# A trunk layer on one core: the gate and feed-forward products taken as 512, 256 and 384 columns over high and low token parts that lie side by side

## The chip, the core and the metric

The kernel runs on one core of a Trainium2 chip. The metric is the device time of one execution in microseconds (us). The median of three runs before the change is 2050.86 us (2049.79 to 2052.56). The engines are called as the profile calls them: PE is TensorE's matmul and PEld its weight load, DVE is VectorE, ACT is ScalarE, POOL is GpSimd, SP is SyncE, whose queue issues nearly all DMAs.

## What is computed

One transformer-like layer over 384 tokens of width 2048: 128 context tokens (the prompt) and 256 latent tokens. All of it is float32.

```
def trunk_layer(x, cond, lw, attend):
    sh1, sc1, g1, sh2, sc2, g2 = modulation(cond, w_mod_l, b_mod_l)
    h = rms_norm(x, n1) * (1 + sc1) + sh1
    q, k, v, u = project_in(h, w_in_l, qg_l, kg_l)
    attn = attend(q, k, v)
    x = x + g1 * token_mixing(h, attn, u, w_na_proj_l, w_fnet_proj_l, w_gate_l, w_o_l)
    h2 = rms_norm(x, n2) * (1 + sc2) + sh2
    x = x + g2 * swiglu(h2, w_gu_l, w_down_l)
    return x, k, v

def token_mixing(h, attn, u, w_na_proj, w_fnet_proj, w_gate, w_o):
    na = attn.reshape(b, t, D_NA) @ w_na_proj
    fn = fourier_mix(u) @ w_fnet_proj
    g_na, g_fn = jnp.split(jax.nn.sigmoid(h @ w_gate), 2, axis=-1)
    return (g_na * na + g_fn * fn) @ w_o

def swiglu(h, w_gate_up, w_down):
    a, g = jnp.split(h @ w_gate_up, 2, axis=-1)
    return (jax.nn.silu(g) * a) @ w_down
```

The change bears on `h @ w_gate` (2048 by 4096) and on `h @ w_gate_up` (2048 by 11264).

## The kernel before

**High and low parts.** A float32 matrix is split into a high part H, rounded to the type fp32r, and a low part L = x - H (`split`, L142 to L144: a cast on ACT, a subtraction on DVE). A product of two float32 matrices is then three fp32r products added up in PSUM: H by H, H by L and L by H (`mm3`, L146 to L149; the fourth, L by L, is left out). In `mm3` the second argument is the stationary operand, 128x128, and the third streams past it. The first two products have the same stationary operand. The profile names the streaming operand first: `mm<-hL,wh` is wh stationary and hL streaming.

**Weights.** All weight matrices come through one list of units in the order of their use (`units`). A unit is two row blocks by 512 columns (512 KB): loaded by SP into `wraw` (four buffers, L187), split into `wh` and `wl` (three buffers each) in `split_unit`, used by PE. `next_unit` is called once for each unit of products: it splits a later unit, lets the other work of the stage take its paced steps (`Paced`: rows of the modulation, attention, splits of activations), and asks for one more load. So the order on ACT, DVE and SP is fixed by the place of each call in the Python text, and each engine takes its instructions in that order.

**PSUM.** Accumulators are tiles of 128 partitions by 512 float32 columns, one bank each. From the mixing stage on, `acc_tile` hands out seven of them in rotation (`new_ring`); the gate stage takes its four from the four `mm` tiles alone.

**Stages**, by the time at which their products stand in the trace: the input projection (to 333 us), where tokens are stationary and 512 weight columns stream; the gates (to 676), eight times eight units, in which the Fourier and attention branches are woven by `front`; the mixing stage (to 811), the two branch projections, each gated; the output projection (to 948); the feed-forward part. There `FF_PARTS` cuts 44 blocks of 128 hidden channels into parts of 8, 8, 8, 8, 8 and 4. In a part, groups of four channel blocks take two halves of eight units (half 1: the SiLU branch, half 0: the factor), and then the part's rows of `w_down` are applied in units of 512 columns with the activations (`cH`, `cL`) stationary. The very first group (to 1018 us) uses the unnormed tokens with two more columns (386 wide, `wide`, `late_norm`); it is not touched by the change. From then on `h2` is there as `hH` and `hL`.

**What the change touches.** In the gates and in the later feed-forward groups the weights are stationary and the 384 tokens stream, so that the result has channels on partitions and tokens in columns. `new_h` (L232) gives the two token tiles of a row block, each 128x384. In the gate loop (L1018 to L1036) a result of 384 columns is copied out of PSUM (`gst`, L1032) by ACT, or by DVE for two of the four tiles in some of the rounds, and stored in DRAM (`s_gate`, by ACT's queue). `load_gates` (L1053) loads four results at once in the mixing stage, a sigmoid is taken at the third unit (L1084), the product with the branch follows (L1092). In the feed-forward part a result goes through SiLU on ACT (L1319) or a multiplication on DVE (L1321), straight from PSUM. `split_act` (L1248) then splits the activations; in the last part, which has four blocks, its step stands directly behind each multiplication (`work.step()`), elsewhere it is spread over the following units.

Of the kernel before, what the change touches and what calls it, by code (L numbers as in the profile page):

```python
# [19 lines left out]
P = 128  # L20
# [12 lines left out]
CH = 512  # L33
# [68 lines left out]
def trunk_kernel(ctx: ExitStack, tc: tile.TileContext, io: dict):  # L102
# [35 lines left out]
    def nm(s):  # L138
        return f"{s}{next(ids)}"
# [6 lines left out]
    def mm3(out, aH, aL, bH, bL, start, stop):  # L146
        nc.tensor.matmul(out, aH, bH, start=start, stop=False)  # L147
        nc.tensor.matmul(out, aH, bL, start=False, stop=False)  # L148
        nc.tensor.matmul(out, aL, bH, start=False, stop=stop)  # L149

    def warm_sqrt():

        warm = small.tile([P, 1], F32, tag="warm", bufs=1, name=nm("warm"))
        nc.scalar.activation(out=warm, in_=ones[:, 0:1], func=AF.Sqrt)
# [72 lines left out]
    rq = consts.tile([P, NT, NH], F32, tag="rq", name="rq")  # L227

    hH = [None] * KT
    hL = [None] * KT  # L230

    def new_h(kt):  # L232
        hH[kt] = hpool.tile([P, TOK], F32R, tag=f"tH{kt}", name=nm(f"hH{kt}_"))
        hL[kt] = hpool.tile([P, TOK], F32R, tag=f"tL{kt}", name=nm(f"hL{kt}_"))
        return hH[kt], hL[kt]

    s_qkvu = [dram.tile([P, NT, CH], F32, tag=f"sq{i}", name=f"s_qkvu{i}") for i in range(8)]
    s_gate = [dram.tile([P, 4, TOK], F32, tag=f"sg{i}", name=f"s_gate{i}") for i in range(8)]
    s_row = {
# [26 lines left out]
    with ExitStack() as ph:  # L266
# [751 lines left out]
        for fc8 in range(8):  # L1018
            po = [mm_tile() for _ in range(4)]
            sts = []  # L1020
            for u in range(0, KT, 2):
                wH, wL = next_unit()
                for f in range(4):
                    s = slice(f * P, (f + 1) * P)
                    if f == 2:
                        mid_unit()
                    for kk in range(2):
                        k = u + kk
                        mm3(po[f][:, :TOK], wH[:, kk, s], wL[:, kk, s], hH[k], hL[k], k == 0, k == KT - 1)
                    if u == KT - 2:  # L1030
                        st = gst.tile([P, TOK], F32, tag="st", name=nm("gst"))
                        (nc.vector.tensor_copy if f < 2 and any(soft) else nc.scalar.copy)(st, po[f][:, :TOK])  # L1032
                        sts.append(st)
# [19 lines left out]
        def load_gates(f4, i):  # L1053
            g = bs.tile([P, 4, TOK], F32, tag="gl", bufs=3, name=nm("gl"))
            nc.sync.dma_start(g, s_gate[i * 4 + f4])
            return g
# [19 lines left out]
        for f4 in range(4):  # L1076
            gl = [None, None]
            for i, bH, bL in ((1, fH, fL), (0, aH, aL)):
                _, gl[i] = gates.take()
                po = [acc_tile() for _ in range(4)]  # L1080
                for u in range(0, 8, 2):
                    wH, wL = next_unit()
                    if u == 4:
                        nc.scalar.activation(out=gl[i], in_=gl[i], func=AF.Sigmoid)  # L1084
                    for f in range(4):
# [170 lines left out]
    def late_norm(o, sg, half):  # L1256
# [10 lines left out]
        return b  # L1267

    def silus(sg, bs):
        for f, b in enumerate(bs):  # L1270
# [19 lines left out]
    for part, nf in enumerate(FF_PARTS):  # L1290
# [5 lines left out]
        for c4 in range(nf // 4):  # L1296
            for half in (1, 0):
                po = [acc_tile() for _ in range(4)]
                bs = []
                for u in range(0, KT, 2):  # L1300
                    wH, wL = next_unit()
                    for f in range(4):
                        s = slice(f * P, (f + 1) * P)
                        for kk in range(2):
                            k = u + kk
                            xH, xL = wide(k) if facc is None else (hH[k], hL[k])
                            mm3(
                                po[f][:, : xH.shape[1]], wH[:, kk, s], wL[:, kk, s], xH, xL, k == 0, k == KT - 1
                            )
                        if u < KT - 2:  # L1310
# [5 lines left out]
                        if facc is None:  # L1316
                            bs.append(late_norm(po[f], sg[:, f], half))
                        elif half:
                            nc.scalar.activation(out=sg[:, f], in_=po[f][:, :TOK], func=AF.Silu)  # L1319
                        else:  # L1320
                            nc.vector.tensor_mul(sg[:, f], sg[:, f], po[f][:, :TOK])  # L1321
                            if nf == 4:
                                work.step()
# [84 lines left out]
```

## Time and profile before

| | |
|---|---|
| median of three runs | 2050.86 us |
| the profiled execution | 2052.19 us |
| its span in the trace | 2050.4 us |
| input projection and modulation, 0 to 335 us | PE busy 318.77 us |
| gates, Fourier and attention, 335 to 676 us | PE busy 337.80 us |
| mixing, 676 to 810 us | PE busy 134.00 us |
| output projection, 810 to 987 us | PE busy 176.23 us |
| feed-forward, 1018 to 2013 us | PE busy without a gap |
| last down projection, 2013 to 2050.4 us | PE busy 33.01 us |

In the page and the views, a group's line gives busy time, mean ns of one instruction, then the engine's idle time ahead of it and what ended it. A row of the timeline is start, duration, engine, line, what is written and read, and shape. A row of the windows view gives, for a stretch, its length, each engine's busy time with its number of instructions in brackets, the granted clock of PE, the share of time that the DMA engines worked, and GB/s. A matmul's duration holds its latency; consecutive ones overlap, so that the distance of two starts is what one costs.

### The profile page before, as it was taken

What the parts mean: (1) busy time and instruction counts of PE and PEld (TensorE: products, weight loads), DVE (VectorE), ACT (ScalarE), POOL (GpSimd) and SP (SyncE); (2) the same over time, 40 slices, a digit from 0 to 9 for tenths busy, and PEclk for the clock granted to TensorE, in tenths of its full rate; (3) what the DMA queues carried; (4) which work ended last, traced back from release to release, by engine and by line L of the source; (5) the groups of instructions that cost most, each with busy time, mean ns of one, the idle gap of its engine ahead of it and who ended that gap; (6) DMA issues with size and microseconds to landing.
All of it is one profiled execution on the core that took longest, in us unless ns stands there. A gap on an engine that the chain in (4) does not pass through costs nothing.

```text
span 2050.4 us, 27528 instructions
## 1 busy us (share of the span) xinstructions
PE 2025.8 (99%) x10986; PEld 1843.8 (90%) x10986; DVE 1248.0 (61%) x1528; ACT 757.9 (37%) x1135; POOL 43.1 (2%) x92
## 2 busy tenths in 40 slices
PE   7999999999999999999999999999999999999999
PEld 4668788999999999889998999899989998999897
DVE  4746889788987777765854444545454334333456
ACT  4433232456665434334523332222222232223222
POOL 1000000000001000010000000000000000000000
PEclk9999999999999999999999999999999999999999
DMA  9996979677776776754455555455554444444453
GB/s 332 328 338 222 309 232 315 215 217 212 228 212 181 258 248 194 250 168 154 124 167 156 152 163 155 144 153 155 155 163 134 124 129 127 129 128 123 136 163 123
DMA packets 220384, 390.46 MB, mean 190 GB/s; under 512 B 28464, under 2 KB 77632, under 8 KB 220256
## 3 DMA queue, kind: packets, MB, share of 16 engines
q1 hardware_dynamic: 213088, 382.13, 59.5%
q10 hardware_dynamic: 4672, 6.31, 0.9%
q8 instruction: 86, 1.41, 0.3%
q0 software_dynamic: 2496, 0.27, 0.1%
q14 instruction: 42, 0.34, 0.1%
HBM read 371.81 MB, written 20.51 MB: 191 GB/s over the span
## 4 chain that ended last, share of the span: by engine, by line
PE 94%; DMA 3%; DVE 2%; ACT 1%; issue 0%; SPq 0%; ACTq 0%; DVEq 0%
PE mm L147 19%; PE mm L149 19%; PE mm L148 19%; PE at L147 11%; PE at L149 11%; PE at L148 11%; PE at L404 1%; DMA wm<-in_w_mod 1%; DMA wraw<-in_w_in 1%; PE at L893 1%; PE at L979 1%; PE at L958 1%; DMA wmr<-in_w_mod 1%; DVE accr L329 0%; DMA xc<-in_x_prompt 0%
## 5 line engine op out<-in xcount | busy, mean ns | idle before, releaser
L144 DVE TENSOR_TENSOR wl<-wraw,wh 128x1024 fp32r<-128x1024 f32 (+1 forms) x464 | 559.1, 1205 | 668.5 <-ACT wh L143 667.3
L143 ACT CAST wh<-wraw 128x1024 fp32r<-128x1024 f32 (+1 forms) x464 | 480.9, 1038 | 1032.0 <-PE at L148 272.9
L147 PE MATMUL mm<-hH,wh 128*128 128x384 f32 x1152 | 389.4, 338 | 2.4 <-DVE gst L1032 2.4
L149 PE MATMUL mm<-hH,wl 128*128 128x384 f32 x1152 | 385.5, 335 | 0.0
L148 PE MATMUL mm<-hL,wh 128*128 128x384 f32 x1152 | 385.2, 334 | 0.0
L329 DVE SCALAR_TENSOR_TENSOR accr<-wmr,csz,accr 128x1024 f32<-128x1024 f32 x240 | 304.8, 1278 | 5.2 <-DMA wmr<-in_w_mod 5.1
L147 PEld LDWEIGHTS mm<-hH,wh 128*128 128x128 f32 x1152 | 216.3, 188 | 8.1 <-issue 4.3
L148 PEld LDWEIGHTS mm<-hL,wh 128*128 128x128 f32 x1152 | 216.4, 188 | 0.0
L149 PEld LDWEIGHTS mm<-hH,wl 128*128 128x128 f32 x1152 | 216.2, 188 | 0.0
L147 PE MATMUL at<-hH,wh 128*128 128x384 f32 x640 | 213.9, 334 | 0.0
L149 PE MATMUL at<-hH,wl 128*128 128x384 f32 x640 | 213.9, 334 | 0.0
L148 PE MATMUL at<-hL,wh 128*128 128x384 f32 x640 | 213.8, 334 | 0.0
L147 PE MATMUL mm<-wh,hH 128*128 128x512 f32 x404 | 160.8, 398 | 1.9 <-ACT hH L548 1.2
L148 PE MATMUL mm<-wl,hH 128*128 128x512 f32 x404 | 158.1, 391 | 2.8 <-DVE wl L144 2.8
L149 PE MATMUL mm<-wh,hL 128*128 128x512 f32 x404 | 158.4, 392 | 0.7 <-DVE hL L144 0.4
L147 PE MATMUL mm<-wh,cH 128*128 128x512 f32 x352 | 137.1, 389 | 0.0
L149 PE MATMUL mm<-wh,cL 128*128 128x512 f32 x352 | 137.0, 389 | 0.0
L148 PE MATMUL mm<-wl,cH 128*128 128x512 f32 x352 | 137.0, 389 | 0.0
L147 PEld LDWEIGHTS at<-hH,wh 128*128 128x128 f32 x640 | 120.1, 188 | 1.0 <-ACT wh L143 0.8
L148 PEld LDWEIGHTS at<-hL,wh 128*128 128x128 f32 x640 | 120.1, 188 | 0.2
L149 PEld LDWEIGHTS at<-hH,wl 128*128 128x128 f32 x640 | 120.1, 188 | 0.0
L147 PEld LDWEIGHTS mm<-wh,hH 128*128 128x128 f32 x404 | 76.0, 188 | 25.6 <-issue 3.1
(283 smaller groups left out, 2633.5 us busy)
## 6 DMA issues: line engine op xcount, KB each, us to landing
wraw<-in_w_gate_up SPq DMA_DIRECT2D x176, 512.0 KB, 3.7
wmr<-in_w_mod SPq DMA_DIRECT2D x128, 512.0 KB, 4.9
wraw<-in_w_down SPq DMA_DIRECT2D x88, 512.0 KB, 3.7
wraw<-in_w_gate SPq DMA_DIRECT2D x64, 512.0 KB, 4.3
wm<-in_w_mod SPq DMA_DIRECT2D x80, 384.0 KB, 6.7
wraw<-in_w_in SPq DMA_DIRECT2D x56, 512.0 KB, 5.8
wraw<-in_w_o SPq DMA_DIRECT2D x32, 512.0 KB, 4.7
wraw<-in_w_fnet_proj SPq DMA_DIRECT2D x16, 512.0 KB, 4.9
```

The source lines that it names most:

```text
L143: nc.scalar.copy(H, x)
L144: nc.vector.tensor_sub(L, x, fr(H))
L147: nc.tensor.matmul(out, aH, bH, start=start, stop=False)
L148: nc.tensor.matmul(out, aH, bL, start=False, stop=False)
L149: nc.tensor.matmul(out, aL, bH, start=False, stop=stop)
L329: nc.vector.scalar_tensor_tensor(out=acc[:, cnd], in0=wm, scalar=sc, in1=acc[:, cnd], op0=ALU.mult, op1=ALU.add)
L404: nc.tensor.matmul(pm[q : q + 32, :w], csz[:, k, :], wm[:, ty, kk + par, :], start=k < 2, stop=k >= KT - 2, tile_position=(0, q), skip_gro ...
L893: nc.tensor.matmul(po[j][:, cols], qx[rows[j], q], kx[rows[j], k], start=i == 0, stop=i == 2, tile_position=(j * HD, 0),)
L958: nc.tensor.transpose(o[:, i * P : (i + 1) * P], sc[:, j, c0 : c0 + P], ident)
L979: nc.tensor.matmul(po[j][:, CTX:TOK].rearrange("p (t q) -> p t q", t=2), w[1 + kc], x.rearrange("p (t b) q -> p t b q", t=2)[:, :, 2 * kc ...
```

## The change

The high and low tokens of a row block become one tile of 128 x 2 x 384, so that `b` = [H | L] is 768 columns in one piece. `mm3_wide` multiplies with it: the stationary high weights by the first 512 columns (H of all tokens and L of the 128 context tokens) into the whole bank, the high weights by the other 256 (L of the latent tokens) onto columns 128 to 383, and the low weights by the 384 of H onto columns 0 to 383. A result then lies in 512 columns, of which the last 128 still have to be added to the first 128.

For the gates all 512 columns are copied and stored; the mixing stage loads the 384 and the remaining 128 columns apart (`load_rest`, at a half's first unit), adds them on DVE, and goes on as before. In the feed-forward part `two_parts` copies the last 128 columns to SBUF on ACT (`fold`), adds the first 128 on DVE, and SiLU or the multiplication is done in two pieces, of 256 columns from PSUM and 128 from `fold`.

```
@@ -148,6 +148,13 @@
         nc.tensor.matmul(out, aH, bL, start=False, stop=False)
         nc.tensor.matmul(out, aL, bH, start=False, stop=stop)
 
+    def mm3_wide(out, aH, aL, b, start, stop):
+
+
+        nc.tensor.matmul(out, aH, b[:, :CH], start=start, stop=False)
+        nc.tensor.matmul(out[:, CH - TOK : TOK], aH, b[:, CH:], start=False, stop=False)
+        nc.tensor.matmul(out[:, :TOK], aL, b[:, :TOK], start=False, stop=stop)
+
     def warm_sqrt():
 
         warm = small.tile([P, 1], F32, tag="warm", bufs=1, name=nm("warm"))
@@ -226,16 +233,18 @@
     qg8 = consts.tile([P, 1], F32, tag="qg8", name="qg8")
     rq = consts.tile([P, NT, NH], F32, tag="rq", name="rq")
 
+    hx = [None] * KT
     hH = [None] * KT
     hL = [None] * KT
 
     def new_h(kt):
-        hH[kt] = hpool.tile([P, TOK], F32R, tag=f"tH{kt}", name=nm(f"hH{kt}_"))
-        hL[kt] = hpool.tile([P, TOK], F32R, tag=f"tL{kt}", name=nm(f"hL{kt}_"))
+        h = hpool.tile([P, 2, TOK], F32R, tag=f"t{kt}", name=nm(f"h{kt}_"))
+        hH[kt], hL[kt] = h[:, 0], h[:, 1]
+        hx[kt] = h.rearrange("p i t -> p (i t)")
         return hH[kt], hL[kt]
 
     s_qkvu = [dram.tile([P, NT, CH], F32, tag=f"sq{i}", name=f"s_qkvu{i}") for i in range(8)]
-    s_gate = [dram.tile([P, 4, TOK], F32, tag=f"sg{i}", name=f"s_gate{i}") for i in range(8)]
+    s_gate = [dram.tile([P, 4, CH], F32, tag=f"sg{i}", name=f"s_gate{i}") for i in range(8)]
     s_row = {
         ty: [dram.tile([1, D], F32, tag=f"row{ty}{c}", name=f"s_row{ty}{c}") for c in range(2)] for ty in (2, 3, 4, 5)
     }
@@ -1026,10 +1035,10 @@
                         mid_unit()
                     for kk in range(2):
                         k = u + kk
-                        mm3(po[f][:, :TOK], wH[:, kk, s], wL[:, kk, s], hH[k], hL[k], k == 0, k == KT - 1)
+                        mm3_wide(po[f], wH[:, kk, s], wL[:, kk, s], hx[k], k == 0, k == KT - 1)
                     if u == KT - 2:
-                        st = gst.tile([P, TOK], F32, tag="st", name=nm("gst"))
-                        (nc.vector.tensor_copy if f < 2 and any(soft) else nc.scalar.copy)(st, po[f][:, :TOK])
+                        st = gst.tile([P, CH], F32, tag="st", name=nm("gst"))
+                        (nc.vector.tensor_copy if f < 2 and any(soft) else nc.scalar.copy)(st, po[f])
                         sts.append(st)
             for f, st in enumerate(sts):
                 nc.scalar.dma_start(s_gate[fc8][:, f], st)
@@ -1052,7 +1061,12 @@
 
         def load_gates(f4, i):
             g = bs.tile([P, 4, TOK], F32, tag="gl", bufs=3, name=nm("gl"))
-            nc.sync.dma_start(g, s_gate[i * 4 + f4])
+            nc.sync.dma_start(g, s_gate[i * 4 + f4][:, :, :TOK])
+            return g
+
+        def load_rest(f4, i):
+            g = bs.tile([P, 4, CH - TOK], F32, tag="gr", name=nm("gr"))
+            nc.sync.dma_start(g, s_gate[i * 4 + f4][:, :, TOK:])
             return g
 
         behind.append(Paced(split_a()))
@@ -1080,7 +1094,11 @@
                 po = [acc_tile() for _ in range(4)]
                 for u in range(0, 8, 2):
                     wH, wL = next_unit()
+                    if u == 0:
+                        rest = load_rest(f4, i)
                     if u == 4:
+                        g = gl[i][:, :, : CH - TOK]
+                        nc.vector.tensor_add(g, g, rest)
                         nc.scalar.activation(out=gl[i], in_=gl[i], func=AF.Sigmoid)
                     for f in range(4):
                         s = slice(f * P, (f + 1) * P)
@@ -1266,6 +1284,13 @@
                 )
         return b
 
+    def two_parts(o):
+
+        v = actp.tile([P, P], F32, tag="fold", bufs=4, name=nm("fold"))
+        nc.scalar.copy(v, o[:, TOK:])
+        nc.vector.tensor_add(v, v, o[:, :P])
+        return (slice(P, TOK), o[:, P:TOK]), (slice(0, P), v)
+
     def silus(sg, bs):
         for f, b in enumerate(bs):
             for c, sl in ((0, slice(0, CTX)), (1, slice(CTX, TOK))):
@@ -1303,10 +1328,10 @@
                         s = slice(f * P, (f + 1) * P)
                         for kk in range(2):
                             k = u + kk
-                            xH, xL = wide(k) if facc is None else (hH[k], hL[k])
-                            mm3(
-                                po[f][:, : xH.shape[1]], wH[:, kk, s], wL[:, kk, s], xH, xL, k == 0, k == KT - 1
-                            )
+                            if facc is None:
+                                mm3(po[f][:, :XW], wH[:, kk, s], wL[:, kk, s], *wide(k), k == 0, k == KT - 1)
+                            else:
+                                mm3_wide(po[f], wH[:, kk, s], wL[:, kk, s], hx[k], k == 0, k == KT - 1)
                         if u < KT - 2:
                             continue
                         if half and f == 0:
@@ -1315,11 +1340,14 @@
                             work = Paced(split_act(c4 * 4, sg, cH, cL), 2)
                         if facc is None:
                             bs.append(late_norm(po[f], sg[:, f], half))
-                        elif half:
-                            nc.scalar.activation(out=sg[:, f], in_=po[f][:, :TOK], func=AF.Silu)
                         else:
-                            nc.vector.tensor_mul(sg[:, f], sg[:, f], po[f][:, :TOK])
-                            if nf == 4:
+                            parts = two_parts(po[f])
+                            for sl, o in parts:
+                                if half:
+                                    nc.scalar.activation(out=sg[:, f, sl], in_=o, func=AF.Silu)
+                                else:
+                                    nc.vector.tensor_mul(sg[:, f, sl], sg[:, f, sl], o)
+                            if not half and nf == 4:
                                 work.step()
                 if facc is None and half:
                     behind.append(Paced(silus(sg, bs)))
```

The instructions in the built programs, at three places. The lines of the changed kernel have other numbers: L147 to L149 of `mm3` stay, `mm3_wide` is L154 to L156. First PE, in the last gate-up unit of the last feed-forward part, two row blocks of one result tile (`mm_...`), before:

```order
L147 MATMUL mm_16651<-hH_1519_9019,wh_16579 128x384
L148 MATMUL mm_16651<-hL_1520_9020,wh_16579 128x384
L149 MATMUL mm_16651<-hH_1519_9019,wl_16580 128x384
L147 MATMUL mm_16651<-hH_1524_9055,wh_16579 128x384
L148 MATMUL mm_16651<-hL_1525_9056,wh_16579 128x384
L149 MATMUL mm_16651<-hH_1524_9055,wl_16580 128x384
```

and after:

```order
L154 MATMUL mm_16931<-h_1495_9011,wh_16843 128x512
L155 MATMUL mm_16931<-h_1495_9011,wh_16843 128x256
L156 MATMUL mm_16931<-h_1495_9011,wl_16844 128x384
L154 MATMUL mm_16931<-h_1499_9046,wh_16843 128x512
L155 MATMUL mm_16931<-h_1499_9046,wh_16843 128x256
L156 MATMUL mm_16931<-h_1499_9046,wl_16844 128x384
```

Each group of three stays at its place with the same operands; the widths are other ones, and the streaming operand is one tile `h`.

Second DVE behind those products, where the tiles are folded, multiplied (`sg`) and split (`cL`), before:

```order
L144 TENSOR_TENSOR wl_16881<-wraw_16760,wh_16880 128x1024
L1321 TENSOR_TENSOR sg_16627<-sg_16627,mm_16650 128x384
L144 TENSOR_TENSOR cL_16894<-sg_16627,cH_16893 128x384
L1321 TENSOR_TENSOR sg_16627<-sg_16627,mm_16651 128x384
L144 TENSOR_TENSOR cL_16905<-sg_16627,cH_16904 128x384
L1321 TENSOR_TENSOR sg_16627<-sg_16627,at_16652 128x384
```

and after:

```order
L144 TENSOR_TENSOR wl_17161<-wraw_17040,wh_17160 128x1024
L1291 TENSOR_TENSOR fold_17172<-fold_17172,mm_16930 128x128
L1349 TENSOR_TENSOR sg_16891<-sg_16891,mm_16930 128x256
L1349 TENSOR_TENSOR sg_16891<-sg_16891,fold_17172 128x128
L144 TENSOR_TENSOR cL_17178<-sg_16891,cH_17177 128x384
L1291 TENSOR_TENSOR fold_17187<-fold_17187,mm_16931 128x128
L1349 TENSOR_TENSOR sg_16891<-sg_16891,mm_16931 128x256
L1349 TENSOR_TENSOR sg_16891<-sg_16891,fold_17187 128x128
L144 TENSOR_TENSOR cL_17193<-sg_16891,cH_17192 128x384
```

An addition stands ahead of each multiplication, which is now two; the split of the next unit's weights that follows them in the queue moves back behind them. On ACT at the same place, before:

```order
L143 CAST wh_16880<-wraw_16760 128x1024
L143 CAST cH_16893<-sg_16627 128x384
L143 CAST cH_16904<-sg_16627 128x384
L143 CAST cH_16915<-sg_16627 128x384
L143 CAST cH_16926<-sg_16627 128x384
```

and after:

```order
L143 CAST wh_17160<-wraw_17040 128x1024
L1290 COPY fold_17172<-mm_16930 128x128
L143 CAST cH_17177<-sg_16891 128x384
L1290 COPY fold_17187<-mm_16931 128x128
L143 CAST cH_17192<-sg_16891 128x384
```

A copy of the fold columns, which waits for the end of the tile's products, stands ahead of each cast `cH`.

Third SP at the begin of the mixing stage, before:

```order
L1055 DMA gl_6552<-s_gate_95 128x1536
L1055 DMA gl_6554<-s_gate_91 128x1536
L1055 DMA gl_6556<-s_gate_96 128x1536
L187 DMA wraw_6571<-in_w_na_proj 128x2x512
L299 DMA wmr_6602<-in_w_mod 128x1024
L187 DMA wraw_6608<-in_w_na_proj 128x2x512
```

and after:

```order
L1064 DMA gl_6536<-s_gate_95 128x4x384
L1064 DMA gl_6538<-s_gate_91 128x4x384
L1064 DMA gl_6540<-s_gate_96 128x4x384
L194 DMA wraw_6555<-in_w_na_proj 128x2x512
L1069 DMA gr_6557<-s_gate_95 128x4x128
L308 DMA wmr_6588<-in_w_mod 128x1024
L194 DMA wraw_6594<-in_w_na_proj 128x2x512
```

The gate load is cut to 384 columns in each of four rows, and a load of the remaining 128 (`gr`) stands between two weight loads (`wraw`) and a modulation load (`wmr`), once for each of the eight halves of the stage.

## The prediction

> **What bounds the kernel now.** I read the page first: its busy shares and the chain that ended last, then the windows view by stage.
>
> ```profile
> span 2050.4 us, 27528 instructions
> PE 2025.8 (99%) x10986; PEld 1843.8 (90%) x10986; DVE 1248.0 (61%) x1528; ACT 757.9 (37%) x1135; POOL 43.1 (2%) x92
> PE 94%; DMA 3%; DVE 2%; ACT 1%; issue 0%; SPq 0%; ACTq 0%; DVEq 0%
> core 0: us, PE busy (x) PEld busy (x) DVE busy (x) ACT busy (x) POOL busy (x), PEclk, DMA share, GB/s
> 335.00:676.00 341.00, 337.80 (x2112) 326.30 (x2111) 278.90 (x363) 188.32 (x395) 14.08 (x29) 1.00 0.72 221
> 676.00:810.00 134.00, 134.00 (x776) 132.91 (x775) 106.06 (x127) 55.06 (x62) 4.37 (x9) 1.00 0.73 242
> 1150.00:2013.00 863.00, 863.00 (x4626) 815.65 (x4625) 388.46 (x396) 249.88 (x278) 6.29 (x13) 1.00 0.48 142
> ```
>
> The last three rows are the gate stage (335 to 676), the mixing stage (676 to 810) and most of the feed-forward part. TensorE is the chain: 94% of it, at a granted clock of 1.00, without any idle time in the mixing and feed-forward rows and with 3.2 us idle in the gate row. So the time is a count of products, each at the distance from one product's start to the next. The products that the change touches are these.
>
> ```profile
> L147 PE MATMUL mm<-hH,wh 128*128 128x384 f32 x1152 | 389.4, 338 | 2.4 <-DVE gst L1032 2.4
> L147 PE MATMUL at<-hH,wh 128*128 128x384 f32 x640 | 213.9, 334 | 0.0
> L147 PEld LDWEIGHTS mm<-hH,wh 128*128 128x128 f32 x1152 | 216.3, 188 | 8.1 <-issue 4.3
> ```
>
> 1152 + 640 = 1792 groups of three (each of L147, L148 and L149 has these counts): 512 in the gates, 1280 in the feed-forward part. The 334 ns of a row are its latency, not its price, since the products overlap. The price is the distance of starts, from the timeline of PE. For 384 columns, the first and the last of a stretch with twelve products from start to start:
>
> ```profile
> 1449.95 0.33 PE L147 MATMUL mm<-hH,wh 128*128 128x384 f32 x1
> ...
> 1452.03 0.33 PE L147 MATMUL at<-hH,wh 128*128 128x384 f32 x1
> ```
>
> 2.08 us / 12 = 173.3 ns, so a group costs 520.0 ns and the 1792 groups 932 us, 45% of the span. For 512 columns, again twelve from start to start:
>
> ```profile
> 1300.05 0.39 PE L147 MATMUL mm<-wh,cH 128*128 128x512 f32 x1
> ...
> 1302.77 0.39 PE L147 MATMUL at<-wh,cH 128*128 128x512 f32 x1
> ```
>
> 2.72 us / 12 = 226.7 ns. The difference of 53.4 ns for 128 columns is 0.417 ns a column, so a product costs about 13 ns plus 0.417 ns a column.
>
> **The change, part by part.**
>
> *The groups.* Three products and three weight loads stay three. The columns are 512 + 256 + 384 = 1152, as 3 x 384 before. If the price is linear in columns, nothing changes. The unknown is the 256. The trace has such products where the Fourier stage interleaves with the gates:
>
> ```profile
> 363.50 0.34 PE L149 MATMUL mm<-hH,wl 128*128 128x384 f32 x1
> 363.68 0.28 PE L147 MATMUL at<-latH,uH 128*128 128x258 f32 x1
> ...
> 364.39 0.28 PE L147 MATMUL at<-ctxH,uH 128*128 128x256 f32 x1
> 364.50 0.28 PE L148 MATMUL at<-ctxL,uH 128*128 128x256 f32 x1
> 364.62 0.28 PE L149 MATMUL at<-ctxH,uL 128*128 128x256 f32 x1
> 364.74 0.34 PE L147 MATMUL mm<-hH,wh 128*128 128x384 f32 x1
> ```
>
> A 256 followed by other weights costs 0.12 us, twice (364.50 to 364.62 to 364.74); the six of 258 before them take (364.39 - 363.68) / 6 = 118 ns; the line gives 120. The new 256 is followed by a product with other weights (aL), so I take 120. Steps between widths cost nothing extra there: 384 to 258 is 0.18. From 512 down:
>
> ```profile
> 1149.64 0.39 PE L149 MATMUL at<-wh,cL 128*128 128x512 f32 x1
> 1149.87 0.33 PE L147 MATMUL at<-hH,wh 128*128 128x384 f32 x1
> ...
> 852.31 0.39 PE L149 MATMUL at<-wh,hL 128*128 128x512 f32 x1
> 852.54 0.38 PE L1152 MATMUL at<-ident,x 128*128 128x128 f32 x2
> ```
>
> 0.23 to a 384 and 0.23 to a 128-column transpose, against 226.7: no extra, with the rows' rounding an estimated 6 ns at most. So a group becomes 226.7 + 120 + 173.3 = 520.0 ns, and **this term is 0 us**. Its bounds: with the mean of the three 256 starts, 0.35 us / 3 = 116.7 ns, it is -3.3 ns x 1792 = -6 us; with 6 ns more for the step from 512 it is +11 us.
>
> *Gate results.* 32 copies out of PSUM grow from 384 to 512 columns, their stores by a third, eight loads of 128 columns (SP) and eight VectorE adds of 128x512 come in the mixing stage. Prices from rows:
>
> ```profile
> L1032 ACT COPY gst<-mm 128x384 f32<-128x384 f32 x28 | 12.8, 483 | 7.5 <-PE mm L149 7.4
> L678 ACT COPY acc<-mm 128x512 f32<-128x512 f32 x16 | 9.2, 587 | 10.6 <-PE mm L149 10.1
> L680 DVE COPY acc<-mm 128x512 f32<-128x512 f32 x8 | 5.5, 690 | 12.7 <-PE mm L149 12.7
> PE mm L147 <- DVE gst L1032: 2.4, 2, 1.5
> ```
>
> On ScalarE 28 x 104 ns = 2.9 us; on VectorE 4 copies and 8 adds of 690 are about 6 us more; together some 9 us of engine work. It lies beside TensorE's 475 us of the two stages, where VectorE has 62 and 28 us free and the DMA engines 27%. Only the copies that PE waits for are open: two waits, 2.4 us, on VectorE's copies; a copy longer by 0.14 us adds about 0.3 us. The loads wait in SP's queue ahead of weight loads, but each is issued at u == 0 and added at u == 4, two units of 4.2 us later. I take **+0.3 us**; bounds 0 and, if all of it lay open, +9.
>
> *Folding in the feed-forward part.* Each of 80 results gets a ScalarE copy and a VectorE add of 128x128, and its SiLU or product falls into pieces of 256 and 128 columns.
>
> ```profile
> L873 ACT CAST kH<-at 128x128 fp32r<-128x128 f32 x8 | 2.1, 264 | 0.0
> L878 DVE TENSOR_TENSOR kL<-at,kH 128x128 fp32r<-128x128 f32 x8 | 2.2, 280 | 0.0
> L144 DVE TENSOR_TENSOR pt<-at,pt 128x256 fp32r<-128x256 f32 x8 | 3.3, 415 | 0.0
> ```
>
> A product result then takes 264 + 280 + 415 + 280 = 1.24 us instead of 0.55. Cover: of the seven PSUM tiles in rotation a half uses four, so its first tile is wanted by the next half 3 x 1.04 us after the half's end and was complete 3 x 1.04 us before it: 6.2 us for 1.24 and for what else queues. Behind the copies on ScalarE stands the split of a weight unit, needed two units (8.3 us) later and 2.3 us long. VectorE is 45% and ScalarE 29% busy in that row. So 0, but for one place: in the last part (four tiles, L1321) folding and splitting follow each other directly and the down projection waits for them.
>
> ```profile
> 2010.86 0.55 DVE L1321 TENSOR_TENSOR sg<-sg,mm 128x384 f32<-128x384 f32 x1
> 2011.99 0.56 DVE L144 TENSOR_TENSOR cL<-sg,cH 128x384 fp32r<-128x384 f32 x1 [0.58 <-ACT cH L143]
> 2012.47 0.55 DVE L1321 TENSOR_TENSOR sg<-sg,mm 128x384 f32<-128x384 f32 x1
> 2013.23 0.40 PE L149 MATMUL at<-wh,cL 128*128 128x512 f32 x1
> 2013.61 0.50 PE L147 MATMUL at<-wh,cH 128*128 128x512 f32 x1
> ```
>
> A tile takes 1.6 us there (2010.86 to 2012.47), and PE's second k, which needs the second tile's cH, starts 0.38 after the product before instead of 0.23: the place is already late by 0.15. With 0.28 for the add and 0.14 for the cut (0.28 + 0.415 against 0.55) a tile takes 2.0; the second tile's cH comes 2 x 0.42 = 0.85 us later. PE then catches nothing up: **+0.85 us**; bounds 0.4 (ScalarE's part hidden) and 1.7 (the third and fourth tile late too).
>
> *Sum.* 0 + 0.3 + 0.85 = +1.2 us. The profiled execution took 2052.19 us, 1.8 more than its span, and becomes 2053.4; the median of the runs shown, 2050.86, is 1.3 below the profiled one, so I predict **2052.0**. What a measurement here can tell from no change is about 0.2%, 4.1 us.
>
> **Rivals.** *Weight loads bind the 256 (slower).* Every product has its load (x1152 in both rows), even where L147 and L148 share weights, and one lasts 188 ns. A 256 could then not be shorter than the 173.3 of a 384, and the group would cost 226.7 + 173.3 + 173.3: +53.3 ns x 1792 = +96 us, 2147. Against it: 256 columns with a load each start 0.12 apart at 364.50. Chance 0.03. [...]
>
> *The step from 512 to 256 costs 6 ns (slower).* 1792 x 6 = +11 us, 2063. The 852.54 row bears at most that. Chance 0.08.
>
> *VectorE and ScalarE hold PE up (slower).* VectorE is at 82% and 79% in the gate and mixing rows; if adds and longer copies delay the split of weights whenever the queue is full, the 9 us come through: 2061. It decides where the split's slack of some 6 us is gone; the 0.00 idle in the mixing row speaks against it. Chance 0.11.
>
> *The second product of a weight is cheaper (faster).* 364.39 to 364.50 is 0.11, both with uH. If the 256 costs between 110 and 116.7, the gain is 6 to 18 us: 2034 to 2046. But it is the product ahead of a repeated load that is short there, and here that is the 512; and L147 to L148 repeat the weights before the change too, at the same 173. Chance 0.08.
>
> **How the numbers follow.** The forecast holds 0.70, by itself 2048 to 2055. Faster by over 0.2% is the last rival alone, 0.08; slower the other three, 0.22; within, 0.70. The range takes in the bounds -6 and +11: 2046 to 2063, and leaves out the loads' rival, most of the cheap second product and the edge of VectorE's.
>
> **What would show it.** In the after profile: starts of L154, L155 and L156 at 0.227, 0.12 and 0.173, sum 0.52; PE without idle time in the feed-forward rows; the first rows of the last down projection later by about 0.9; the same 10986 loads. Wrong would be a 256 at 0.17, a 512 ahead of a 256 above 0.23, fewer loads than products, or new waits of PE for `fold`, `gl` or `wl`.

## The result, and the profile after

The changed kernel is slower by 0.86%: its median is 2067.4 us (four executions, 2066.29 to 2072.23) against 2050.32 for the kernel before beside it, a ratio of 1.0086 [1.0068, 1.0104]. It lies 4.4 us above the range. The first two rows are from the page, the others from the windows view of the changed kernel (length, busy time of PE, PEld, DVE, ACT and POOL, clock, DMA share, GB/s): the gates, then mixing and output projection cut at their first products, then the feed-forward part.

```profile
span 2070.5 us, 27824 instructions
PE 2033.1 (98%) x10986; PEld 1774.1 (86%) x10986; DVE 1273.7 (62%) x1656; ACT 779.5 (38%) x1255; POOL 43.1 (2%) x92
335.00:676.00 341.00, 335.77 (x2099) 303.91 (x2099) 278.76 (x362) 188.70 (x392) 14.08 (x29) 1.00 0.73 225
679.95:823.82 143.87, 138.00 (x778) 134.45 (x778) 108.69 (x132) 53.63 (x62) 4.37 (x9) 0.99 0.73 238
823.82:967.85 144.03, 139.81 (x623) 113.46 (x622) 91.60 (x114) 51.68 (x83) 5.35 (x11) 0.98 0.60 194
1150.00:2013.00 863.00, 863.00 (x4600) 766.25 (x4599) 400.40 (x486) 269.75 (x387) 6.29 (x13) 1.00 0.47 143
```

PE is still without a gap in the feed-forward part, where 2560 of the 3584 new wide products are. It is idle for 5.9 us in mixing (143.87 - 138.00) and 4.2 in the output projection, and the granted clock falls there (0.99 and 0.98), in two stages whose products the change does not touch. From the first product of a stage to that of the next, in the timelines of both kernels:

| stage | before, us | after, us | difference |
|---|---|---|---|
| up to the gates | 333.30 | 335.04 | +1.7 |
| gates | 342.97 | 344.91 | +1.9 |
| mixing | 134.34 | 143.87 | +9.5 |
| output projection | 137.63 | 144.03 | +6.4 |
| first feed-forward group, 386 wide | 69.72 | 69.71 | 0.0 |
| feed-forward, to the last down projection | 994.81 | 994.70 | -0.1 |
| last down projection | 37.63 | 38.24 | +0.6 |

The sum is 20.1 us, the difference of the spans (2070.5 - 2050.4). The medians differ by 17.1: the profiled execution of the changed kernel is the longest of its four. Two executions of the experiments below took far longer than the others of their kernel (2872.02 us in e4, 5204.01 in e12), and the medians given there leave them out. The 1.7 us ahead of the gates are not the change's: the input projection, alike in all kernels of this study, takes between 305.3 and 310.1 us in them. So 15.9 of some 18 us lie in mixing and output projection. The waits view of the changed kernel from 676 to 860 us (engine, line and what waited; what ended it; us in total, times, longest):

```profile
DVE wl L144 <- ACT wh L143: 36.8, 22, 4.8
ACT gl L1102 <- DVE gl L1101: 25.2, 7, 5.8
ACT gl L1102 <- DMA wmr<-in_w_mod: 6.8, 1, 6.8
PE mm L147 <- ACT wh L143: 3.9, 2, 3.8
PE mm L147 <- DVE gl L1110: 3.8, 2, 2.2
PE mm L149 <- DVE wl L144: 1.6, 3, 0.6
```

The second and third rows are new. All eight sigmoids (L1102, ACT) wait, 32 us in all, for the addition of the remaining columns (L1101, DVE); the third row is one of them, put down to a DMA, though it starts as the addition of 749.98 us ends. Before, the sigmoid needed only the load of the gates, and did not wait. It is ACT's timeline that shows what this does; the last half before the output projection, first in the kernel before, then in the changed one (start, duration; in brackets the idle time ahead and its end):

```profile
802.32 1.05 ACT L143 CAST wh<-wraw 128x1024 fp32r<-128x1024 f32 x1 [3.10 <-PE at L148]
803.27 1.48 ACT L1084 ACTIVATE gl<-gl 128x1536 f32<-128x1536 f32 x1
806.48 1.05 ACT L143 CAST wh<-wraw 128x1024 fp32r<-128x1024 f32 x1 [1.72 <-PE at L148]
```

```profile
815.49 1.05 ACT L143 CAST wh<-wraw 128x1024 fp32r<-128x1024 f32 x1 [3.36 <-PE at L148]
822.31 1.49 ACT L1102 ACTIVATE gl<-gl 128x1536 f32<-128x1536 f32 x1 [5.78 <-DVE gl L1101]
823.71 1.03 ACT L143 CAST wh<-wraw 128x1024 fp32r<-128x1024 f32 x1
```

And VectorE's timeline of the changed kernel at the same place:

```profile
816.79 1.22 DVE L144 TENSOR_TENSOR wl<-wraw,wh 128x1024 fp32r<-128x1024 f32 x1
...
820.26 1.28 DVE L338 SCALAR_TENSOR_TENSOR accr<-wmr,csz,accr 128x1024 f32<-128x1024 f32 x1
821.59 0.69 DVE L1101 TENSOR_TENSOR gl<-gl,gr 128x512 f32<-128x512 f32 x1
824.77 1.23 DVE L144 TENSOR_TENSOR wl<-wraw,wh 128x1024 fp32r<-128x1024 f32 x1 [2.49 <-ACT wh L143]
```

In these rows of the kernel before, ACT waits only for PE to free a buffer: its casts are ahead as far as the buffers allow, and the next cast starts 4.16 us after the last (806.48 - 802.32). After, ACT stands still for 5.78 us, since the addition lies behind splits (L144) and modulation rows (L338) in VectorE's queue; the next cast comes 8.22 us after the last (823.71 - 815.49). Then VectorE, through with its queue, waits 2.49 us for that cast. Each engine has waited for the other in this half, and the lead that both had over PE is gone. What PE sees of it at the begin of the output projection, in its timeline of the changed kernel:

```profile
831.79 0.39 PE L149 MATMUL mm<-wh,h 128*128 128x512 f32 x1
835.93 0.79 PE L147 MATMUL mm<-wh,h 128*128 128x512 f32 x1 [3.76 <-ACT wh L143]
837.20 0.79 PE L148 MATMUL mm<-wl,h 128*128 128x512 f32 x1 [0.47 <-DVE wl L144]
...
841.20 0.63 PE L148 MATMUL mm<-wl,h 128*128 128x512 f32 x1
841.63 0.63 PE L149 MATMUL mm<-wh,h 128*128 128x512 f32 x1
...
842.44 0.39 PE L148 MATMUL mm<-wl,h 128*128 128x512 f32 x1
842.67 0.39 PE L149 MATMUL mm<-wh,h 128*128 128x512 f32 x1
```

PE waits for weights, and then starts products 0.43 us apart (841.20 to 841.63) where 0.23 is the price (842.44 to 842.67): its granted clock is 0.50 from 835.55 to 842.38 us, and ten products from 837.79 us take 2.0 us more. In mixing the clock falls once, to 0.50 from 702.43 to 705.85 us, for another 1.5 us; some 2 us of the 9.5 there go into restarts (a wait of 2.18 us keeps the next start 2.34 late, and the product behind it another 0.12; there are seven such waits). Of the 5.9 us that PE stands idle in mixing, 3.8 are not waits for weights but for the multiplications (L1110) that free its PSUM tiles, and they come from the same loop between the two queues. VectorE's timeline of the changed kernel in the first half, and the row of PE that waits there:

```profile
694.88 0.69 DVE L1101 TENSOR_TENSOR gl<-gl,gr 128x512 f32<-128x512 f32 x1 [0.91 <-DMA gr<-s_gate]
698.06 1.23 DVE L144 TENSOR_TENSOR wl<-wraw,wh 128x1024 fp32r<-128x1024 f32 x1 [2.49 <-ACT wh L143]
...
701.45 0.55 DVE L1110 TENSOR_TENSOR gl<-gl,mm 128x384 f32<-128x384 f32 x1
```

```profile
702.05 0.44 PE L147 MATMUL mm<-aH,wh 128*128 128x384 f32 x1 [2.18 <-DVE gl L1110]
```

The split waits for the cast behind the sigmoid, and the multiplication stands behind the split.

### The profile page after: what moved, and what is told of

The parts are those of the page before. It is cut to its first block, busy times and chain, and to the rows that moved or that the text cites. A ratio compares the mean times of both kernels' runs of the same rounds, so it can differ in the third digit from the quotient of the medians.

```text
span 2070.5 us, 27824 instructions
## 1 busy us (share of the span) xinstructions
PE 2033.1 (98%) x10986; PEld 1774.1 (86%) x10986; DVE 1273.7 (62%) x1656; ACT 779.5 (38%) x1255; POOL 43.1 (2%) x92
## 4 chain that ended last, share of the span: by engine, by line
PE 59%; DVE 0%; ACT 0%; issue 0%
PE at L154 7%; PE mm L154 7%; PE mm L148 6%; PE mm L149 6%; PE mm L147 6%; PE mm L156 5%; PE at L156 5%; PE mm L155 4%; PE at L155 4%; PE at L147 3%; PE at L149 3%; PE at L148 3%; PE at L1170 0%; PE at L347 0%; DVE wl L144 0%; DVE x L1380 0%
## 5 line engine op out<-in xcount | busy, mean ns | idle before, releaser
L144 DVE TENSOR_TENSOR wl<-wraw,wh 128x1024 fp32r<-128x1024 f32 (+1 forms) x464 | 558.8, 1205 | 637.0 <-ACT wh L143 631.6
L154 PE MATMUL mm<-h,wh 128*128 128x512 f32 x1152 | 454.0, 394 | 4.3 <-DVE gst L1041 2.7
L156 PE MATMUL mm<-h,wl 128*128 128x384 f32 x1152 | 386.3, 335 | 0.0
L155 PE MATMUL mm<-h,wh 128*128 128x256 f32 x1152 | 322.7, 280 | 0.0
L338 DVE SCALAR_TENSOR_TENSOR accr<-wmr,csz,accr 128x1024 f32<-128x1024 f32 x240 | 304.8, 1278 | 6.3 <-DMA wmr<-in_w_mod 6.2
L156 PEld LDWEIGHTS mm<-h,wl 128*128 128x128 f32 x1152 | 215.5, 187 | 48.3
L154 PE MATMUL at<-h,wh 128*128 128x512 f32 x640 | 249.8, 390 | 0.0
L154 PEld LDWEIGHTS mm<-h,wh 128*128 128x128 f32 x1152 | 217.6, 189 | 10.1 <-issue 4.3
L155 PEld LDWEIGHTS mm<-h,wh 128*128 128x128 f32 x1152 | 216.4, 188 | 0.0
L156 PE MATMUL at<-h,wl 128*128 128x384 f32 x640 | 214.4, 335 | 0.0
L155 PE MATMUL at<-h,wh 128*128 128x256 f32 x640 | 179.2, 280 | 0.0
L147 PE MATMUL mm<-wh,h 128*128 128x512 f32 x404 | 161.8, 401 | 5.7 <-ACT wh L143 3.8
L149 PE MATMUL mm<-wh,h 128*128 128x512 f32 x404 | 159.3, 394 | 0.7 <-DVE h L144 0.4
L156 PEld LDWEIGHTS at<-h,wl 128*128 128x128 f32 x640 | 119.7, 187 | 26.6
L149 PE MATMUL mm<-wh,cL 128*128 128x512 f32 x352 | 137.1, 389 | 0.0
L147 PE MATMUL mm<-wh,cH 128*128 128x512 f32 x352 | 137.0, 389 | 0.0
L154 PEld LDWEIGHTS at<-h,wh 128*128 128x128 f32 x640 | 120.9, 189 | 1.0 <-ACT fold L1290 0.8
L155 PEld LDWEIGHTS at<-h,wh 128*128 128x128 f32 x640 | 120.1, 188 | 0.2
L147 PEld LDWEIGHTS mm<-wh,h 128*128 128x128 f32 x404 | 76.7, 190 | 30.0 <-issue 4.4
```

The costliest lines, as they stand in the source:

```text
L144: nc.vector.tensor_sub(L, x, fr(H))
L154: nc.tensor.matmul(out, aH, b[:, :CH], start=start, stop=False)
L155: nc.tensor.matmul(out[:, CH - TOK : TOK], aH, b[:, CH:], start=False, stop=False)
L156: nc.tensor.matmul(out[:, :TOK], aL, b[:, :TOK], start=False, stop=stop)
L338: nc.vector.scalar_tensor_tensor(out=acc[:, cnd], in0=wm, scalar=sc, in1=acc[:, cnd], op0=ALU.mult, op1=ALU.add)
```

## The experiments

The theory after the result: the wait of the sigmoid for the addition costs the 16 us, not the wide products and not the added work. The rivals: the work (VectorE's additions, the longer copies), the loads, the wide products. Each of the kernels e1 to e12 was timed in three rounds against the kernel before. Stage lengths as above, from each kernel's profile; the feed-forward part took 994.69 to 994.81 us in all.

| kernel | ratio to before | gates | mixing | output projection |
|---|---|---|---|---|
| before | | 342.97 | 134.34 | 137.63 |
| after | 1.0086 [1.0068, 1.0104] | 344.91 | 143.87 | 144.03 |
| e1_gates_narrow | 1.0003 [0.9994, 1.0013] | 343.16 | 134.35 | 137.66 |
| e3_apart | 1.0017 [1.0008, 1.0027] | 345.99 | 134.38 | 137.61 |
| e4_no_add | 1.0015 [1.0006, 1.0025] | 344.72 | 134.35 | 137.61 |
| e5_before_max | 1.0070 [1.0053, 1.0087] | 343.06 | 142.66 | 144.33 |
| e6_pool_add | 1.0072 [1.0057, 1.0087] | 344.46 | 144.41 | 141.93 |
| e7_sigmoid_later | 1.0022 [1.0012, 1.0031] | 345.74 | 134.34 | 137.64 |
| e8_add_earlier | 1.0050 [1.0035, 1.0065] | 346.59 | 137.93 | 139.78 |
| e9_last_apart | 1.0045 [1.0028, 1.0062] | 344.71 | 141.81 | 137.69 |
| e10_pool_ahead | 1.0026 [1.0016, 1.0035] | 345.35 | 138.03 | 137.61 |
| e11_dve_ahead | 1.0025 [1.0015, 1.0034] | 344.98 | 136.82 | 137.66 |
| e12_narrow_results | 1.0002 [0.9993, 1.0012] | 342.70 | 134.35 | 137.62 |

**e1: only the feed-forward part wide.** In the gate loop the products, copies, stores and loads are those of before:

```
-                        mm3_wide(po[f], wH[:, kk, s], wL[:, kk, s], hx[k], k == 0, k == KT - 1)
+                        mm3(po[f][:, :TOK], wH[:, kk, s], wL[:, kk, s], hH[k], hL[k], k == 0, k == KT - 1)
```

> The gates are as before the change (three products of 384, no fold, no extra loads); only the feed-forward part is wide. All theories put the loss at the gates' results, so all expect 2051 us (the +0.6 of the last down projection stays, ratio 1.000 to 1.001) and the mixing stage back at 134.3 us. 2060 or more would mean that the feed-forward part or the merged token tile costs time that the trace hides.

2051.3 us against 2050.92. The 1280 wide groups, the folding and the later tail together cost nothing that can be told from no change; all of the loss hangs on the gates.

**e3: the addition kept, but nobody waits for it.**

```
-                        g = gl[i][:, :, : CH - TOK]
-                        nc.vector.tensor_add(g, g, rest)
+                        nc.vector.tensor_add(rest, rest, rest)
                         nc.scalar.activation(out=gl[i], in_=gl[i], func=AF.Sigmoid)
```

> The fold addition is replaced by an addition of the loaded 128 columns to themselves, same shape, same wait for the load, same place on VectorE; the gates lack the folded part (left out of the result). ScalarE's sigmoid no longer depends on VectorE. Theory A (ScalarE must wait for VectorE's queue and loses its lead over it): 2051 to 2054 us. Theory B (eight more VectorE operations of 0.69 us in a nearly full queue): stays near 2067 us. Theory C (more DMA traffic, SP's queue, longer copies): stays near 2067 us.

**e4: no addition.** The line with `tensor_add` and the one ahead of it go; the loads stay.

> The fold addition of the gates is left out (the context tokens' gates lack the low part), the loads of 128 columns, the longer copies and stores stay. Theory A and theory B: 2051 to 2053 us. Theory C (DMA traffic, SP's queue, longer copies): stays near 2067 us.

**e5: the wait alone, in the kernel before.**

```
                     if u == 4:
+                        g = gl[i][:, :, : CH - TOK]
+                        nc.vector.tensor_tensor(out=g, in0=g, in1=g, op=ALU.max)
                         nc.scalar.activation(out=gl[i], in_=gl[i], func=AF.Sigmoid)
```

> The kernel before, with one VectorE operation of 128x512 added ahead of each sigmoid that writes the maximum of 128 of its columns with themselves, so that the values stay. No wide products, no additional DMA. Theory A: the loss appears without the change, 2062 to 2068 us, and ScalarE's idle time ahead of the sigmoid on VectorE is 25 us as in the changed kernel. Theory B: also a loss, of like size. Theory C: 2051 us.

These three tell work and wait apart. With the same VectorE instruction at the same place and the same load, but no dependence (e3), mixing and output projection are back at 134.38 and 137.61 us; leaving the addition out (e4) gives no more. With the dependence alone (e5: narrow products, no added load) they are at 142.66 and 144.33, and the kernel is 14.5 us slower (2065.42 - 2050.92). Its waits view from 676 to 860 us has the same new row:

```profile
ACT gl L1086 <- DVE gl L1085: 30.6, 8, 6.8
...
PE mm L147 <- ACT wh L143: 3.6, 1, 3.6
PE mm L147 <- DVE gl L1094: 3.6, 2, 2.0
```

In the same view of e3 no sigmoid waits for VectorE, and PE waits once, as in the kernel before:

```profile
PE mm L148 <- DVE wl L144: 0.8, 1, 0.8
```

What is left in e3 and e4, 2.6 and 2.7 us over the kernel before, stands in the gate stage (345.99 and 344.72 against 342.97); e12 below takes it up.

**e6: the addition on GpSimd, at the half's first unit**, so that the sigmoid does not depend on VectorE's queue:

```
                         rest = load_rest(f4, i)
-                    if u == 4:
                         g = gl[i][:, :, : CH - TOK]
-                        nc.vector.tensor_add(g, g, rest)
+                        nc.gpsimd.tensor_add(g, g, rest)
+                    if u == 4:
                         nc.scalar.activation(out=gl[i], in_=gl[i], func=AF.Sigmoid)
```

> The changed kernel with the gates' fold addition on GpSimd, issued where the 128 columns are loaded (u == 0); the sigmoid at u == 4 as it is. Theory A (the loss is ScalarE waiting for VectorE's queue): ScalarE finds the addition done, the mixing stage is back at 134.4 us, 2052 to 2055 us in all with the 2 to 3 us that the wider copies of the gate stage cost in the runs without the addition. If instead any dependence of the sigmoid on a second engine is what costs, or GpSimd slows VectorE, it stays above 2058.

A miss: 2065.95 us. The waits view of e6 shows why:

```profile
POOL gl L1100 <- DMA gr<-s_gate: 77.1, 6, 17.1
...
ACT gl L1102 <- POOL gl L1100: 24.8, 5, 5.5
```

The sigmoid still waits, now for GpSimd, and GpSimd for the load `gr`. In the last half, SP's queue (start, time to issue) and ACT's timeline of e6:

```profile
809.90 0.37 SPq L194 DMA_DIRECT2D wraw<-in_w_o  x1
810.36 0.52 SPq L1069 DMA_DIRECT2D gr<-s_gate  x1
```

```profile
811.53 1.06 ACT L143 CAST wh<-wraw 128x1024 fp32r<-128x1024 f32 x1 [3.11 <-PE at L148]
817.01 1.49 ACT L1102 ACTIVATE gl<-gl 128x1536 f32<-128x1536 f32 x1 [4.42 <-POOL gl L1100]
```

The load stands at the half's first unit in the program, but in SP's queue it is behind weight loads, whose buffers come free with VectorE's splits (SP waits 119.1 us for them in the changed kernel from 660 to 860 us); it is issued 1.2 us ahead of the cast that stands before the sigmoid. Such loads land 4.5 to 8.3 us after their issue (median 5.7), and the addition takes 1.29 us. The other engine had removed one link of the chain; behind it was the load.

**e7: the sigmoid one unit later.** The addition stays at the third unit:

```
                         nc.vector.tensor_add(g, g, rest)
+                    if u == 6:
                         nc.scalar.activation(out=gl[i], in_=gl[i], func=AF.Sigmoid)
```

> The changed kernel with the addition at u == 4 as it is and the sigmoid one unit later, at u == 6. The distance grows by one unit of VectorE's queue (some 4.2 us), against waits of 3.4 us on average (25.2 us in seven). Theory A: most of the loss goes, 2053 to 2058 us, with ScalarE's wait for the addition under 8 us in total.

Two sigmoids wait for 4.3 us in all instead of eight for 32, ACT keeps its lead, and both stages are back at 134.34 and 137.64. Among the kernels that have wide gates with the folded part in the result, this has the lowest median, 2054.83 us, and it is still above the kernel before.

**e8: the addition one unit earlier**, at `u == 2`, the sigmoid at the third unit.

> The changed kernel with the addition one unit earlier, at u == 2, and the sigmoid at u == 4 as it is. Same distance as with the later sigmoid, but now the addition stands one unit behind the issue of its load. Theory A: ScalarE's wait goes, but VectorE may wait for the load (some 6 us to landing) in its place: 2053 to 2060 us. If the place of the sigmoid and not its distance from the addition counted, it would differ from the later sigmoid by more than 5 us.

2061.55 us, 5.9 below the changed kernel and above what was expected: VectorE now waits 14.1 us for the load (DVE L1101 on `gr`), and the sigmoids still 19.4 for VectorE.

**e9: the dependence kept in the first three groups of mixing, not in the fourth.**

```
-                        nc.vector.tensor_add(g, g, rest)
+                        if f4 < 3:
+                            nc.vector.tensor_add(g, g, rest)
+                        else:
+                            nc.vector.tensor_add(rest, rest, rest)
```

> The changed kernel; in the last group of four (the last two of eight halves) the addition goes to the loaded columns alone, so that these two sigmoids do not wait (the folded part of the last 512 channels' gates is left out). Theory A with a lead that is lost half by half and carried into the next stage: the output projection is back at 137.6 us from 144.0, the mixing stage keeps a part of its 9.5 us, 2055 to 2061 us in all. If the 6.4 us of the output projection had another cause (late weight loads, the residual loads), they would stay.

Mixing still takes 141.81 us, but the output projection is at 137.69. So its 6.4 us are not its own: they are the lead lost in the last two halves of mixing and paid for when the casts of the mixed results come on top.

**e10 and e11: the load one half earlier**, in two buffers; the addition on GpSimd at the first unit (e10) or on VectorE at the second (e11):

```
+        rests = Ahead(load_rest, [(f4, i) for f4 in range(4) for i in (1, 0)], 1)
...
-                        rest = load_rest(f4, i)
+                        _, rest = rests.take()
+                        rests.more()
```

> The addition on GpSimd at u == 0 as in the run before, but its 128 columns are loaded one half ahead (two buffers). In that run five sigmoids still waited 24.8 us for GpSimd, each time because the load, issued by SP behind a weight load that waits for VectorE's split, landed 5 to 6 us later. Theory A, widened (ScalarE may not wait for anything that is set off only when VectorE reaches this half; the load through SP is such a thing): the waits go, mixing stage 134.4 us, 2052 to 2055 us. If GpSimd as such is in the way, it stays at 2066.

> The addition on VectorE at u == 2 and the sigmoid at u == 4, as in the run with the earlier addition (2061.6 us), but the columns are loaded one half ahead. There VectorE waited 14.1 us for the load and ScalarE 19.4 us for VectorE. Theory A: without the load's part it comes to the time of the later sigmoid (2054.8), 2053 to 2057 us, mixing stage under 135 us. If the place on VectorE alone counted, it stays at 2061.

With both links gone the waits of the sigmoid fall to 3.9 us (e10) and 6.4 (e11), the output projection is whole, and mixing is at 138.03 and 136.82: better than e6 and e8, which had the late load, by 6.4 and 1.1 us, but not where it was expected. In each one wait of PE is left beside the one of the kernel before, 1.8 and 2.2 us, for the multiplications that free PSUM; in e10 the clock falls behind it (0.72 from 697 to 703 us).

**e12: the wide products kept, only their first 384 columns copied, stored and loaded.**

```
-                        st = gst.tile([P, CH], F32, tag="st", name=nm("gst"))
-                        (nc.vector.tensor_copy if f < 2 and any(soft) else nc.scalar.copy)(st, po[f])
+                        st = gst.tile([P, TOK], F32, tag="st", name=nm("gst"))
+                        (nc.vector.tensor_copy if f < 2 and any(soft) else nc.scalar.copy)(st, po[f][:, :TOK])
```

> Wide products, but of the gates' results 384 columns are copied, stored and loaded as before the change (the low part of the context tokens is left out of the gates). It splits the 2 to 3 us that the gate stage still loses in the runs without the addition. If the longer copies and stores cost them: gate stage at 343 us and 2051 to 2052 us in all. If the products of 512 and 256 cost them in that stage (512 groups there have a mean of 237.9 ns ahead of the 256, against 229.1 in the feed-forward part): gate stage at 345 us, 2053 to 2054 us.

2050.86 us against 2050.52, and the gate stage at 342.70. So the 512 wide groups of the gates cost nothing either, and the 2 to 3 us of that stage come from the longer copies and stores together. Where they show, in the waits of the gate stage (330 to 676 us), first of the changed kernel, then of e12:

```profile
PE mm L154 <- DVE gst L1041: 2.7, 2, 1.6
...
PE mm L154 <- ACT gst L1041: 1.7, 1, 1.7
```

```profile
PE mm L154 <- DVE gst L1041: 2.4, 2, 1.5
```

The second of the changed kernel's rows is a wait of PE for a copy on ScalarE, which e12 and the kernel before do not have. Why copies that are 0.11 us longer (a mean of 591 ns on ScalarE against 483) bring ScalarE there 1.7 us late was not followed further, and copies of 512 columns alone, without the stores of 512, were not tried.

## Why the prediction was wrong, step by step

**The groups: right.** PE's timeline of the changed kernel in the feed-forward part:

```profile
1449.23 0.39 PE L154 MATMUL mm<-h,wh 128*128 128x512 f32 x1
1449.46 0.28 PE L155 MATMUL mm<-h,wh 128*128 128x256 f32 x1
1449.57 0.34 PE L156 MATMUL mm<-h,wl 128*128 128x384 f32 x1
...
1451.83 0.39 PE L154 MATMUL mm<-h,wh 128*128 128x512 f32 x1
```

Five groups take 2.60 us, 0.520 each as before: 0.23, 0.11 and 0.18. Over the whole part that is -0.1 us. With it fall the rivals of the bound weight loads, of the step from 512 to 256 and of the cheaper second product. The busy share of the weight loads fell from 90% to 86% of the span, and no time came of it in these traces: the part with most of the wide groups took 994.70 us after 994.81.

**Folding in the feed-forward part: right**, 0 us, PE without a gap.

**The last part's tail: right in mechanism, +0.6 instead of +0.85.** VectorE's timeline of the changed kernel, two tiles apart by one:

```profile
2030.35 0.28 DVE L1291 TENSOR_TENSOR fold<-fold,mm 128x128 f32<-128x128 f32 x1
...
2032.22 0.28 DVE L1291 TENSOR_TENSOR fold<-fold,mm 128x128 f32<-128x128 f32 x1
```

A tile takes 1.87 us, not 2.0: the prediction added durations, and VectorE's instructions start a little before the one ahead has ended. The multiplication behind the first of these additions starts at 2030.55 us, 0.08 us before the addition's end.

**The gate results: the step that failed.** "It lies beside TensorE's 475 us of the two stages, where VectorE has 62 and 28 us free", with +0.3 us for copies that PE waits for and 9 at most. Two things were wrong. The size of the copies' term: the gate stage lost 1.9 us here (1.8 and 3.0 in e4 and e3), since a copy on ScalarE became a new wait of PE of 1.7 us. The +0.3 us had been taken for the waits that were there, on VectorE's copies, and these did grow by that much, from 2.4 to 2.7. And, 15.9 us, the thing left out: the added work was costed as time on an engine, and as a load that must arrive ("each is issued at u == 0 and added at u == 4"), but not as a new edge between two queues. The sigmoid behind the addition was never asked about. It stands in ScalarE's queue ahead of the weight casts, so that the casts for later units now had to wait until VectorE, 79% busy in the row of before, came to the addition. And "two units" was the distance in the program; in e6 SP reached the load only 1.2 us before ScalarE's cast ahead of the sigmoid.

**The rival "VectorE and ScalarE hold PE up"** had the right engines and the right sign, and the wrong price and reason: it let 9 us of work come through. e3 has the work and loses nothing in mixing; e5 has the wait, with eight instructions on VectorE and none of the other work, and loses 14.5 us. The prediction's own signs of being wrong named the place, though: the new waits of PE are on `gl` (3.8 us) and `wl` (1.6 us). Its evidence against, no idle time of PE in the mixing row, said that the lead was enough for what then stood in the queues, not for a wait that takes the lead away eight times.

## What to carry to other kernels

A small instruction put on a busy engine is to be priced by who waits for it, not by its duration (eight of them cost 14.5 us in e5): follow the new dependence into the queue of the consumer, and ask what stands behind the consumer there. The queues did not stand at the same place of the program at one time (in e6 SP issued the load of the first unit 1.2 us ahead of the cast before the third unit's sigmoid), so "two units later" in its text need not be two units in time. Where such an edge is needed, put the consumer later (e7), and start its load earlier (e11), before moving the work to another engine (e6).

## What the runs showed of the hardware

Short gaps were followed by half of PE's clock in some places, and not in others. In the changed kernel an idle time of 2.18 us (ended at 702.05) was followed by products 0.32 us apart instead of 0.17 until 705.8 us, and one of 3.76 us by ten at 0.43 instead of 0.23. The granted clock, the third number from the end in the windows view, was 0.51 behind the second:

```profile
836.00:842.50 6.50, 6.03 (x14) 4.41 (x15) 6.50 (x6) 1.78 (x2) 0.00 (x0) 0.51 0.61 194
```

But in e9 a longer gap at the same place than the first, 2.60 us, was not followed by a slower clock, as its window shows:

```profile
698.00:706.00 8.00, 5.40 (x32) 5.08 (x31) 7.94 (x11) 2.83 (x4) 0.00 (x0) 1.00 0.25 84
```

In e10 one of 1.8 us was, from 1.5 us after it on:

```profile
697.00:703.00 6.00, 5.58 (x23) 5.58 (x24) 6.00 (x8) 1.05 (x1) 0.00 (x0) 0.72 0.25 68
```

So the length of the gap does not decide alone; in e11 one of 2.18 us, as long as the first above, left the clock alone too (1.00 from 676 to 810 us).

The profile's records of the granted clock show the changed kernel at half clock three times between 32 and 2030 us: from 231.39 and from 702.43 us for 3.413 us each, and from 835.55 for 6.827. The falls lie 471.04 and 133.12 us apart, 138 and 39 times the 3.413 us that the first two lasted. In the windows view, the 3.41 us ahead of each fall, and what stands behind the fall:

```profile
227.98:231.39 3.41, 1.15 (x5) 0.96 (x6) 3.41 (x5) 0.62 (x1) 0.00 (x0) 1.00 0.64 181
231.39:234.81 3.42, 3.42 (x10) 2.63 (x9) 3.42 (x3) 0.00 (x0) 0.00 (x0) 0.50 0.51 154
699.02:702.43 3.41, 1.23 (x7) 0.91 (x7) 3.38 (x7) 0.79 (x1) 0.00 (x0) 1.00 0.54 163
702.43:705.85 3.42, 3.42 (x13) 3.42 (x12) 3.42 (x6) 1.05 (x1) 0.00 (x0) 0.50 0.03 7
832.14:835.55 3.41, 0.04 (x1) 0.00 (x0) 2.23 (x5) 1.64 (x3) 0.00 (x0) 1.00 0.01 2
835.55:842.38 6.83, 5.98 (x13) 4.41 (x14) 6.46 (x6) 2.23 (x3) 0.00 (x0) 0.50 0.56 178
```

PE was idle for 2.26, 2.18 and 3.37 us of them (length less busy time). The kernel before has 1.70 us of idle time at the place of the first, in the input projection, and keeps its clock there:

```profile
227.88:231.29 3.41, 1.71 (x7) 1.43 (x8) 3.41 (x4) 0.13 (x1) 0.00 (x0) 1.00 0.59 175
231.29:234.71 3.42, 3.42 (x17) 2.82 (x16) 3.42 (x4) 0.94 (x1) 0.00 (x0) 1.00 0.65 157
```

What made the clock fall at these places and not behind the gaps of e9 and e11 was not shown.
